# Weight buffers 32 bytes longer: the distance between the two operands of a matmul, modulo 256

## The chip, the cores and the metric

The kernel runs on one core of a Trainium2 chip. The metric is the device time of one execution in microseconds (us). Lower is better.

## The reference

Two layers of a decoder trunk on 256 positions of width 2048, in float32. What matters here is how much of it is matrix product with large weights:

```
for l in range(DEPTH):                       # 2 layers
    h = rmsnorm(x, norm_mix[l])
    z = h @ w_in[l]                          # 2048 x 2816
    q, k, v, u_ssm, z_u, z_v = split(z)
    y = concat(rmsnorm(window attention of q, k, v), rmsnorm(S5 scan of u_ssm, with ssm_w_glu),
               rmsnorm(gmlp of z_u, z_v))
    x = x + y @ w_out[l]                     # 2048 x 2048
    h = rmsnorm(x, norm_ffn[l])
    x = x + (silu(h @ w_gate[l]) * (h @ w_up[l])) @ w_down[l]   # 2048 x 5632 twice, 5632 x 2048
return rmsnorm(x, norm_final)
```

## The kernel before

**The dense products.** All large weights come as one stream of halves of 128 x 1024 float32 (512 KB). SyncE's queue brings a half into a `raw` buffer (`pump`, L172, five buffers). ScalarE copies it, rounded to TensorE's short float32 format (fp32r), into a `whi` buffer (`split_hi`, L182). VectorE subtracts: what the rounding left goes into a `wlo` buffer (`split_lo`, L191). There are four `whi` and four `wlo` buffers (`NH`), used in turn, so half number j lies in buffer j modulo 4 of each kind. The activations, transposed, are split in the same way into `xh` and `xl`, or, for the outputs of the three branches and of the FFN, into the two halves of `ya` and `yb`.

`dense` (L283) walks over the halves. A half holds two tiles of 128 x 512 (or four of 128 x 256 for the keys and values), and for each tile `unit` (L273) issues six matmuls: for each of the two blocks of 128 positions, activation-high times `whi` (L279), activation-high times `wlo` (L280), activation-low times `whi` (L281). The activation block of 128 x 128 is the stationary operand (loaded by an LDWEIGHTS of its own before each matmul), the weight tile of 128 x 512 is the moving one. After each tile `tick` lets the side work take a step: transposes (L343), attention (L817, L842, L853), the scan (L585 to L663), so that bursts of small matmuls stand between the dense ones. A half is split two to three halves ahead of its use.

**Where the buffers lie.** Tiles come from pools that lie one behind the other in a partition's memory; each tile takes a multiple of 32 bytes of each partition. First comes `const` (among its tiles, in this order: `x`, `ident`, `identr`, `consts`, `gains`, `sinks`, `nsinks`, `bs`, `dskip`, `prm` and small ones). Then the four pools of `Homes` (L135): everything that has no home of its own (`raw`, `t4`, `qT`, `kT`, `brep`, `pT` and others), then `whi` and `wlo`, then `xh`, `xl`, `ya`, `yb`, then the operands of the scan. Before the change a `whi` or `wlo` buffer has 4096 bytes, `xh` and `xl` 16384 each, and a stationary block starts a multiple of 512 bytes into its tile, a moving one a multiple of 1024. So the first `whi` lies at byte 98048, which is 383 times 256, `xh` lies 8 x 4096 bytes behind it, and the distance from any dense moving operand to any dense stationary operand is a multiple of 256. Of the other operands, `brep` starts on a multiple of 256 as well, as 11008 bytes (43 x 256) lie between its second buffer and the first `whi`; `pT`, `qT` and `kT` start 128 bytes past a multiple (4480 bytes, 17.5 x 256, lie between the first `pT` and the first `whi`).

Of the kernel before, what the change touches and what calls it, by code (L numbers as in the profile page):

```python
# [10 lines left out]
F32 = mybir.dt.float32  # L11
F32R = mybir.dt.float32r
# [3 lines left out]
L = 2  # L16
# [136 lines left out]
class Builder:  # L153
# [27 lines left out]

    def split_hi(self):  # L182
        j = self.n_hi
        h = self.work.tile([128, 1024], F32R, tag="whi", name="whi", bufs=self.NH)
        w = 512 if j < self.FINE else 1024
        for o in range(0, 1024, w):
            self.nc.scalar.activation(out=h[:, o:o + w], in_=self.raw[j][:, o:o + w], func=AF.Copy)  # L187
        self.hi[j] = h
        self.n_hi += 1

    def split_lo(self):  # L191
        j = self.n_lo
        o = self.work.tile([128, 1024], F32R, tag="wlo", name="wlo", bufs=self.NH)
        r = self.raw.pop(j)
        w = 512 if j < self.FINE else 1024
        for i in range(0, 1024, w):
            self.nc.vector.tensor_tensor(out=o[:, i:i + w], in0=r[:, i:i + w], in1=self.hi[j][:, i:i + w], op=ALU.subtract)  # L197
        self.lo[j] = o
        self.n_lo += 1
        self.pump()  # L200
# [764 lines left out]
    def build(self):  # L965
        nc = self.nc
        dr = self.dr
        cst = self.const
# [11 lines left out]
        self.gains = cst.tile([128, L, 48], F32, name="gains")  # L980
        self.sinks = cst.tile([128, L, 16], F32, name="sinks")
        self.nsinks = cst.tile([128, L, 16], F32, name="nsinks")
        self.bs = cst.tile([128, 16], F32, name="bs")[:, 0:4 * L].rearrange("p (a b) -> p a b", b=4)
        self.dskip = cst.tile([128, L, 16], F32, name="dskip")
        self.prm = cst.tile([128, 3, 32], F32, name="prm")
        self.nh = cst.tile([128, 2], F32, name="nh")
# [40 lines left out]
        for l in range(L):  # L1027
# [30 lines left out]
            a = self.acc()  # L1058
            self.dense(a, self.X, D16, ready=ready)
            self.spawn(self.attn(l, 0, a, rs))  # L1060
            a = self.acc()
            self.dense(a, self.X, D16, n=256)
            self.spawn(self.kv(a, rs))
            a = self.acc()
            self.dense(a, self.X, D16)
            self.spawn(self.attn(l, 1, a, rs))
            a = self.acc()
# [3 lines left out]
            a = self.acc()  # L1071
            self.dense(a, self.X, D16)
            self.spawn(self.gmlp_v(l, a, rs))
            a = self.acc()
# [6 lines left out]
            for t in out_tiles():  # L1081
                if t is None:
                    self.need(tssm)
                    a = []
# [24 lines left out]
            for si, s in enumerate(FF_SETS):  # L1109
                self.hev = self.events()  # L1110
                for i, c in enumerate(s):
                    a = self.acc()
                    self.dense(a, self.X, D16, ready=ready)
                    tgte = self.spawn(self.ffn_h(c, i, a, None, rs))
                    a = self.acc()
# [9 lines left out]
                for n in range(4):  # L1125
                    a = self.acc()
# [91 lines left out]
```

## Time and profile before

| what | value |
|---|---|
| runs shown | 2070.57 and 2072.56 us, median 2071.57 |
| the profiled execution: time of the run | 2073.87 us |
| its span, first to last instruction | 2072.0 us |
| granted TensorE clock, mean | 0.993 |
| busy share of the span: TensorE, its weight loads | 99%, 82% |
| VectorE, ScalarE, GpSimd | 58%, 47%, 10% |
| DMA, mean | 187 GB/s |

A row of the timeline gives the start in us from the start of the span, the duration, the engine, the line, the operation, and the tiles (output<-moving,stationary). Matmuls are pipelined: one's recorded duration is longer than the distance to the next one's start, so the pace is read from starts, and durations tell only how one compares with its like. "PEld" is a weight load, which runs beside a matmul.

### The profile page before, as it was taken

To read this page: it belongs to the slowest core of one execution; us is meant where nothing else is said; L and a number is where in the kernel's file an instruction comes from. 1 tells how busy PE (TensorE), PEld (TensorE's weight loads), DVE (VectorE), ACT (ScalarE), POOL (GpSimd) and SP (SyncE) were. 2 spreads that over 40 slices of the span, in tenths; PEclk is the share of its full clock that TensorE was granted. 3 is DMA by queue.
4 is the path that set the end of the run, shared out by engine and by line. 5 is a ranking of instruction groups with operands and counts; after the bars stand their busy time and mean duration, and the time that the engine had idled before them with its cause. 6 is when DMAs were issued, how large, how long until landed. Compare 5 with 4: busy or idle time off the path is not lost.

```text
span 2072.0 us, 25614 instructions
## 1 busy us (share of the span) xinstructions
PE 2041.6 (99%) x9728; PEld 1708.3 (82%) x9728; DVE 1210.9 (58%) x1625; ACT 969.9 (47%) x1289; POOL 206.1 (10%) x196
## 2 busy tenths in 40 slices
PE   8998999999999999999999999999999999999998
PEld 7878888888888888888888888888888888888886
DVE  6898755646555545444556796554455444554445
ACT  6555555444444443344455445544443444434444
POOL 0455004021312100000000010000000000000000
PEclk9998999999999999999999999999999999999999
DMA  7443455566656566665565455555566555555664
GB/s 247 154 142 137 131 185 187 185 217 198 219 197 218 184 219 191 193 192 188 184 218 185 148 186 182 184 189 187 191 192 193 186 192 192 189 194 186 193 194 142
DMA packets 105595, 387.98 MB, mean 187 GB/s; under 512 B 12288, under 2 KB 13056, under 8 KB 104192
## 3 DMA queue, kind: packets, MB, share of 16 engines
q1 hardware_dynamic: 105472, 386.35, 56.8%
q8 instruction: 76, 1.25, 0.2%
q14 instruction: 47, 0.39, 0.1%
HBM read 375.03 MB, written 11.27 MB: 186 GB/s over the span
## 4 chain that ended last, share of the span: by engine, by line
PE 94%; DVE 4%; issue 1%; ACT 0%; DMA 0%; SPq 0%; POOLq 0%; POOL 0%; ACTq 0%; DVEq 0%
PE acc L279 29%; PE acc L281 29%; PE acc L280 29%; PE side L343 2%; DVE wlo L197 1%; PE side L853 1%; PE side L625 1%; PE side L817 1%; DVE st L633 0%; PE side L585 0%; PE side L842 0%; PE side L663 0%; PE side L661 0%; DMA raw<-wts 0%; PE side L658 0%
## 5 line engine op out<-in xcount | busy, mean ns | idle before, releaser
L197 DVE TENSOR_TENSOR wlo<-raw,whi 128x1024 fp32r<-128x1024 f32 (+1 forms) x687 | 855.6, 1250 | 658.9 <-ACT whi L187 657.9
L187 ACT ACTIVATE whi<-raw 128x1024 fp32r<-128x1024 f32 (+1 forms) x687 | 725.8, 1058 | 971.1 <-PE acc L281 919.2
L279 PE MATMUL acc<-whi,xh 128*128 128x512 f32 (+1 forms) x1792 | 704.2, 393 | 1.9 <-ACT whi L187 1.9
L281 PE MATMUL acc<-whi,xl 128*128 128x512 f32 (+1 forms) x1792 | 693.1, 387 | 0.0
L280 PE MATMUL acc<-wlo,xh 128*128 128x512 f32 (+1 forms) x1792 | 692.6, 387 | 0.0
L281 PEld LDWEIGHTS acc<-whi,xl 128*128 128x128 f32 x1792 | 337.6, 188 | 69.4
L279 PEld LDWEIGHTS acc<-whi,xh 128*128 128x128 f32 x1792 | 337.9, 189 | 65.4 <-ACT whi L187 2.3
L280 PEld LDWEIGHTS acc<-wlo,xh 128*128 128x128 f32 x1792 | 338.1, 189 | 63.6 <-DVE wlo L197 0.4
L279 PE MATMUL acc<-whi,ya 128*128 128x512 f32 x512 | 202.0, 394 | 0.0
L280 PE MATMUL acc<-wlo,ya 128*128 128x512 f32 x512 | 199.4, 390 | 0.8 <-DVE wlo L197 0.8
L281 PE MATMUL acc<-whi,ya 128*128 128x512 f32 x512 | 199.5, 390 | 0.0
L279 PE MATMUL acc<-whi,yb 128*128 128x512 f32 x448 | 176.4, 394 | 0.0
L281 PE MATMUL acc<-whi,yb 128*128 128x512 f32 x448 | 174.6, 390 | 0.0
L280 PE MATMUL acc<-wlo,yb 128*128 128x512 f32 x448 | 174.4, 389 | 0.0
L317 POOL TENSOR_TENSOR rs<-ms,nh 128x2 f32<-128x2 f32 (+1 forms) x12 | 12.2, 1013 | 1505.9 <-DVE ms L316 1388.0
L280 PEld LDWEIGHTS acc<-wlo,ya 128*128 128x128 f32 x512 | 96.3, 188 | 20.3 <-DVE wlo L197 1.2
L281 PEld LDWEIGHTS acc<-whi,ya 128*128 128x128 f32 x512 | 96.1, 188 | 20.3
L279 PEld LDWEIGHTS acc<-whi,ya 128*128 128x128 f32 x512 | 96.2, 188 | 19.0
L281 PEld LDWEIGHTS acc<-whi,yb 128*128 128x128 f32 x448 | 84.1, 188 | 17.7
L280 PEld LDWEIGHTS acc<-wlo,yb 128*128 128x128 f32 x448 | 84.2, 188 | 16.8
L279 PEld LDWEIGHTS acc<-whi,yb 128*128 128x128 f32 x448 | 84.1, 188 | 16.8
L379 DVE SCALAR_TENSOR_TENSOR xl<-side,gains,xh 128x256 fp32r<-128x256 f32 x64 | 27.9, 480 | 44.1 <-ACT xh L377 44.1
(223 smaller groups left out, 1280.7 us busy)
## 6 DMA issues: line engine op xcount, KB each, us to landing
raw<-wts SPq DMA_DIRECT2D x684, 512.0 KB, 4.2
saved<-stash SPq DMA_DIRECT2D x4, 1792.0 KB, 6.3
stash<-saved SPq DMA_DIRECT2D x3, 1792.0 KB, 7.6
stashb<-saved SPq DMA_DIRECT2D x2, 1792.0 KB, 8.9
bc<-bc SPq DMA_DIRECT2D x8, 256.0 KB, 4.5
out<-x SPq DMA_DIRECT2D x8, 256.0 KB, 3.0
saved<-stashb SPq DMA_DIRECT2D x1, 1792.0 KB, 7.3
x<-x SPq DMA_DIRECT2D x3, 512.0 KB, 8.2
```

Of the source, the lines that this page charges most:

```text
L187: self.nc.scalar.activation(out=h[:, o:o + w], in_=self.raw[j][:, o:o + w], func=AF.Copy)
L197: self.nc.vector.tensor_tensor(out=o[:, i:i + w], in0=r[:, i:i + w], in1=self.hi[j][:, i:i + w], op=ALU.subtract)
L279: nc.tensor.matmul(out=o, lhsT=a, rhs=wh, start=first, stop=False)
L280: nc.tensor.matmul(out=o, lhsT=a, rhs=wl, start=False, stop=False)
L281: nc.tensor.matmul(out=o, lhsT=b, rhs=wh, start=False, stop=last)
L317: nc.gpsimd.tensor_tensor(out=out, in0=t, in1=self.nh[:, 0:w], op=ALU.pow)
L343: nc.tensor.transpose(ps[:, 256 * kk + 128 * m:256 * kk + 128 * m + 128], parts(2 * b + kk, m), self.ident)
L379: nc.vector.scalar_tensor_tensor(out=o, in0=src, scalar=gain[:, k:k + 1], in1=h.bitcast(F32), op0=ALU.mult, op1=ALU.subtract)
L625: nc.tensor.matmul(out=ps[:, 256 * o + 64 * g:256 * o + 64 * g + 64], lhsT=st[nm][:, 128 * g:128 * g + 128], rhs=U4[:, 4 * ct + g, :])
L817: nc.tensor.matmul(out=ps[:, nk * i:nk * i + nk], lhsT=qT[:, h0 + i], rhs=self.kT[:, j, cq, 0:nk], start=(j == 0), stop=(j == 1))
L853: nc.tensor.matmul(out=ps[:, 64 * i:64 * i + 64], lhsT=pT[:, 128 * (nb * i + b):128 * (nb * i + b) + 128], rhs=self.v[:, b, 64 * cq:64 * c ...
```

## The change

Each `whi` and `wlo` buffer is allocated with 1032 columns, of which the first 1024 are used: it takes 4128 bytes instead of 4096, so successive buffers step by 32 modulo 256. With eight of them `xh` lies 8 x 4128 = 33024 bytes (129 x 256) behind the first `whi`. Counted to any dense stationary operand, the distance modulo 256 of `whi` buffers 0 to 3 becomes 0, 32, 64, 96, and that of `wlo` buffers 0 to 3 becomes 128, 160, 192, 224 (up to the sign). The tile `bs` gets its plain shape of 128 x 2 x 4, 32 bytes where it had 64, so all that lies behind it moves down by 32 bytes; `raw`, `t4` and the rest of the first `Homes` pool then start 32 bytes lower modulo 256. No instruction is added, removed or moved.

```
@@ split_hi
-        h = self.work.tile([128, 1024], F32R, tag="whi", name="whi", bufs=self.NH)
+        h = self.work.tile([128, 1032], F32R, tag="whi", name="whi", bufs=self.NH)[:, 0:1024]
@@ split_lo
-        o = self.work.tile([128, 1024], F32R, tag="wlo", name="wlo", bufs=self.NH)
+        o = self.work.tile([128, 1032], F32R, tag="wlo", name="wlo", bufs=self.NH)[:, 0:1024]
@@ build
-        self.bs = cst.tile([128, 16], F32, name="bs")[:, 0:4 * L].rearrange("p (a b) -> p a b", b=4)
+        self.bs = cst.tile([128, L, 4], F32, name="bs")
```

## Rows read from the trace of the kernel before

**Rows 1.** The page, part 4: shares of the chain that ended last.
```profile
PE 94%; DVE 4%; issue 1%; ACT 0%; DMA 0%; SPq 0%; POOLq 0%; POOL 0%; ACTq 0%; DVEq 0%
```
**Rows 2.** Groups by shape, TensorE: line, operation, tiles, shapes, count | busy us, mean ns.
```profile
L281 PE MATMUL acc<-whi,xl 128*128 128x512 f32 x1728 | 675.0, 391 | 0.0
L280 PE MATMUL acc<-wlo,xh 128*128 128x512 f32 x1728 | 674.5, 390 | 0.0
...
L281 PE MATMUL acc<-whi,ya 128*128 128x512 f32 x512 | 199.5, 390 | 0.0
...
L281 PE MATMUL acc<-whi,yb 128*128 128x512 f32 x448 | 174.6, 390 | 0.0
...
L281 PE MATMUL acc<-whi,xl 128*128 128x256 f32 x64 | 18.1, 283 | 0.0
...
L281 PE MATMUL side<-whi,yb 128*128 128x512 f32 x16 | 6.3, 391 | 0.0
```
**Rows 3.** Timeline of TensorE, first row of an undisturbed dense stretch.
```profile
782.27 0.39 PE L279 MATMUL acc<-whi,ya 128*128 128x512 f32 x1
```
**Rows 4.** Timeline of TensorE, the row 562 matmuls later.
```profile
909.66 0.39 PE L280 MATMUL acc<-wlo,xh 128*128 128x512 f32 x1
```
**Rows 5.** Tile acc, 783 to 909 us: count, duration ns min/median/max.
```profile
L280 PE MATMUL acc<-wlo,xh x71: 389/389/389, 861.4 to 909.0; 128*128 128x512 f32 x71
L281 PE MATMUL acc<-whi,xl x70: 389/389/389, 861.6 to 908.5; 128*128 128x512 f32 x70
```
**Rows 6.** Timeline of TensorE after a burst of transposes.
```profile
289.08 0.60 PE L343 MATMUL side<-ident,x 128*128 128x128 f32 x4
289.44 0.48 PE L279 MATMUL acc<-whi,yb 128*128 128x512 f32 x1
289.75 0.40 PE L280 MATMUL acc<-wlo,yb 128*128 128x512 f32 x1
...
291.84 0.39 PE L280 MATMUL acc<-wlo,yb 128*128 128x512 f32 x1
```
**Rows 7.** Tile acc, 289.8 to 291.7 us: count, duration ns min/median/max.
```profile
L280 PE MATMUL acc<-wlo,yb x3: 387/389/396, 289.8 to 291.1; 128*128 128x512 f32 x3
L281 PE MATMUL acc<-whi,yb x3: 393/395/397, 290.0 to 291.4; 128*128 128x512 f32 x3
```
**Rows 8.** Groups at 1139.72 us: the dense matmul beside which `pT` is loaded.
```profile
L281 PE MATMUL acc<-whi,xl 128*128 128x512 f32 x1 | 0.4, 396 | 0.0
L853 PE MATMUL side<-v,pT 128*128 128x64 f32 x1 | 0.2, 221 | 0.0
```
**Rows 9.** Groups at 542.2 us: the dense matmul beside which `brep` is loaded.
```profile
L281 PE MATMUL acc<-whi,yb 128*128 128x512 f32 x1 | 0.4, 389 | 0.0
L585 PE MATMUL side<-stash,brep 128*128 128x128 f32 x1 | 0.3, 270 | 0.0
```
**Rows 10.** Groups at 144.65 us: a product of `kT` beside which `xh` is loaded.
```profile
L817 PE MATMUL side<-kT,qT 128*128 128x256 f32 x1 | 0.3, 283 | 0.0
```
**Rows 11.** Windows, 782 to 910 us: busy us (count) by engine, clock, DMA share, GB/s.
```profile
782.00:910.00 128.00, 128.00 (x566) 106.00 (x566) 65.24 (x59) 51.09 (x49) 0.00 (x0) 1.00 0.61 193
```
**Rows 12.** The page, part 5: the two splits, busy us, mean ns | idle before, releaser.
```profile
L197 DVE TENSOR_TENSOR wlo<-raw,whi 128x1024 fp32r<-128x1024 f32 (+1 forms) x687 | 855.6, 1250 | 658.9 <-ACT whi L187 657.9
L187 ACT ACTIVATE whi<-raw 128x1024 fp32r<-128x1024 f32 (+1 forms) x687 | 725.8, 1058 | 971.1 <-PE acc L281 919.2
```
**Rows 13.** The page, part 6: DMA issue of the weights, KB each, us to landing.
```profile
raw<-wts SPq DMA_DIRECT2D x684, 512.0 KB, 4.2
```

## The prediction

> **What bounds the kernel now.** I read the chain that ended last first: 94% of the span is TensorE, and no other engine has more than 4% [rows 1]. The groups by shape then say which matmuls: L279, L280 and L281 each issue 1728 + 512 + 448 + 16 matmuls of 512 columns and 64 of 256 [rows 2], where L281 stands for the three lines, that is 3 x 2704 = 8112 wide ones and 192 narrow ones, 8304 in all. So one nanosecond on each dense matmul is 8.3 us, 0.4% of the time.
>
> The pace of these matmuls is the third thing to read, and it is read from starts. In an undisturbed stretch 562 of them take 909.66 - 782.27 = 127.39 us, 226.7 ns each [rows 3, 4], and every one of them has the same duration, 389 ns [rows 5]. In that stretch TensorE is busy without a gap at a granted clock of 1.00, the 2.4 GHz level, VectorE has 65 of 128 us to do and ScalarE 51 [rows 11]. So nothing outside TensorE sets the 226.7 ns. Part of it is streaming: a matmul of 512 columns lasts 389 ns and one of 256 lasts 283 [rows 2, 5], so 256 columns cost 106 ns and 512 cost 212. The other 14.7 ns are the price of going from one matmul to the next, and that is the only thing on the bounding engine that an address can touch.
>
> The fourth thing is that this price is not fixed. After a burst of transposes the dense matmuls do not fall into the 226.7 ns at once: nine starts take 291.84 - 289.75 = 2.09 us, 232.2 ns each, 5.5 ns more [rows 6]. Their durations wander between 387 and 397 ns [rows 7] before they come to rest at 389. What these matmuls compute, and the distance of their operands, is the same as in the steady stretch; only the moment at which the stream began differs. I read this as follows: the two reads of TensorE, the moving one and the weight load that runs beside it, fall on some repeating pattern of the memory, and with all addresses equal modulo 256 the stream settles, within about ten matmuls, at a spot of the pattern that is better than the average.
>
> **What the change does, part by part.**
>
> *The distance.* No instruction changes, so the sum has one large term: 8304 matmuls times the change of the step price. Within a half, the six matmuls of a tile take `whi`, `wlo`, `whi`, `whi`, `wlo`, `whi`; after the change `wlo` lies 128 bytes (modulo 256) from its `whi`, and every half moves both on by 32. The moving address therefore changes its residue at two of three steps, and the stream never has ten equal ones in which to settle. Only matmuls with `whi` buffer 0 keep distance 0: two of three matmuls use `whi`, one buffer of four, 1/6 of all. 5/6 of 8304 is 6920.
>
> For the price the trace has two rows. First, the distance by itself: `pT`, which lies at an odd multiple of 128, is loaded beside a dense matmul of `whi`, and this one lasts 396 ns [rows 8]; `brep`, at a multiple of 256, is loaded beside one of the same kind, and this lasts 389 [rows 9]. Both loads are of 128 x 128 float32. Distance 128 costs 7 ns there. If the price grows with the distance around the ring of 256, 0 at 0 and 7 at 128, the four `whi` distances cost 0, 1.75, 3.5 and 5.25, mean 2.6, and the four `wlo` distances 7, 5.25, 3.5 and 1.75, mean 4.4. Two `whi` and one `wlo` in three give (2 x 2.6 + 4.4) / 3 = 3.2 ns, times 8304: +27 us. Second, the loss of the settled spot: 5.5 ns [rows 3, 4, 6] on 6920 matmuls: +38 us. I take the middle, +32 us.
>
> What bounds it: below, nothing forbids a gain, since 14.7 ns of each step are overhead, and if every distance but 0 removed all of it the change would be worth 6920 x 14.7 = 102 us. Above, the dearest duration seen is 397, 8 ns over 389 [rows 5, 7], which on all 8304 is +66 us.
>
> *The splits.* ScalarE writes `whi` and VectorE reads it and writes `wlo`, now at starts that are multiples of 32 instead of 256. They take 1058 and 1250 ns for a half [rows 12], and TensorE takes 12 x 226.7 = 2720 ns for it. Even at half as slow again VectorE would need 1875 ns, which with the rest of its work in the steady stretch (65 of 128 us for 47 halves, 1388 ns a half [rows 11]) comes to 2013. I cost it at nothing; TensorE's own time hides it, and without that cover a half as slow again would cost 0.6 us for each half that VectorE splits.
>
> *`raw` and the rest, 32 bytes lower.* The transfer of a half lands 4.2 us after its issue [rows 13], and five buffers at 2.72 us each are 13.6 us of room. The DMA engines are busy for 0.61 of the stretch [rows 11]. I cost this at nothing as well. If landings grew past the room, ScalarE's copy would be late next, and then L279.
>
> The sum: the profiled execution took 2073.87 us with a span of 2072.0, 2.3 above the median of the runs shown, 2071.57. 2073.9 + 32 is 2106 for it, and by the median 2071.6 + 32 = **2103 us**, +1.5%.
>
> **Rivals.**
>
> *Nothing happens* (2072 us). A product of `kT`, which lies at an odd multiple of 128, streams while `xh`, at a multiple of 256, is loaded, and it lasts 283 ns [rows 10], as do the narrow dense ones at distance 0 [rows 2]. So distance 128 costs nothing in this place, and rows 8 could owe its 7 ns to the change of operand that follows, not to the distance. Against it: the wandering of rows 6 and 7 shows that the step price depends on how the streams lie in time, and it would be odd if addresses did not enter. The Trainium skill ("SBUF — State Buffer", section "Who interferes with whom") gives TensorE two independent read ports and says that "PE and ACT never wait on anyone". By that rule distance has no price and the time stays at 2072; the trace speaks against the rule in its full width, with 387 to 397 ns for the same matmul [rows 7]. This rival also covers the case that the allocation does not give the distances that the diff asks for.
>
> *The full price everywhere* (2120 to 2140 us). If each change of residue throws the stream to a bad spot and not to an average one, every matmul pays the 7 to 8 ns of rows 7 and 8: 8304 x 7 = 58 us, 2130. It decides against my forecast where the mean step passes 231.6 ns, which is 2113 us. For it: nearly all durations of L281 in rows 7 are 393 to 397. Against it: the same stretch has a 387 too.
>
> *Faster* (about 1970 to 2030 us). Distance 0 could be the worst case, in which the two reads meet in the same place all the time; a spread would then cut into the 14.7 ns. At full effect that is 2072 - 102 = 1970, at half effect 2021; it decides from a mean step below 221.6 ns, 2030 us. For it: the overhead is there, and it is the same 14.7 ns in each of 562 steps, as a collision at a fixed distance would be. Against it: the steady 389 is near the least duration in the trace's irregular stretches (387), and the one pair at another distance in rows 8 is longer, not shorter. The Trainium skill ("TensorE: Matmul & The Clock Gate", section "Step-by-step: what each phase is for") gives 215.7 ns from start to start for 512 columns. By that figure 11 ns of each step could go, an estimate of 91 us on all 8304, 1981; no row here shows so short a step.
>
> **How the numbers follow.** Loss of the settled spot, +20 to +41 us: 0.40. Nothing: 0.20. Full price: 0.30. Faster: 0.10, of which 0.01 for less than 2%. About 2% is what a measurement of this kernel can tell from no change, 2030 to 2113 us. Slower is 0.30, within 2% is 0.40 + 0.20 + 0.01 = 0.61, faster 0.09. The likeliest case gives 2103; its own range is 2092 to 2113. The range for 8 in 10 reaches down past "nothing" to 2055, where a settling at the 387 ns of rows 7 on all matmuls would lie (8304 x 2 = 17 us less), and up to 2140, which is the 8 ns of rows 7 on all (2138); it leaves out the faster rival and the tail of the full price.
>
> **What would show it.** If I am right, the long dense stretches have a mean step of 229 to 231.6 ns where they had 226.7, and the durations of L280 and L281 there are no longer one value but several, repeating with the four buffers. The bursts of side work, the splits, and the landing of `raw` keep their durations, and TensorE stays busy without a gap between 782 and 910 us or its like. A steady 389 there would show the first rival; steps above 231.6 the second; below 221.6 the third. I am wrong in kind if the time goes anywhere else: into waits of L279 for `whi`, or of `whi` for `raw`.

## The result: 2099 us, 1.3% slower, all of it in the step between dense matmuls

The changed kernel takes 2099.38 us (median; 2099.08 to 2099.68), the kernel before 2071.57. The ratio is 1.0135, with a 95% interval from 1.0119 to 1.0152. The profiled execution has a span of 2097.2 us against 2072.0, at a mean granted clock of 0.994 against 0.993.

I read the views in the same order as before. First the shares of the chain that ended last, on the page of the changed kernel (part 4); they answer to [rows 1]:

```profile
PE 94%; DVE 4%; issue 1%; ACT 0%; DMA 0%; SPq 0%; POOLq 0%; POOL 0%; ACTq 0%; DVEq 0%
```

The row is the same, word for word: no wait has taken the place of anything, and TensorE still sets the time. Next, the two splits on the page (part 5: busy us, mean ns, idle before, releaser), which answer to [rows 12]:

```profile
L197 DVE TENSOR_TENSOR wlo<-raw,whi 128x1024 fp32r<-128x1024 f32 (+1 forms) x687 | 856.7, 1252 | 684.3 <-ACT whi L187 683.1
...
L187 ACT ACTIVATE whi<-raw 128x1024 fp32r<-128x1024 f32 (+1 forms) x687 | 724.6, 1056 | 1001.6 <-PE acc L281 945.4
```

They take 1252 and 1056 ns where they took 1250 and 1058. Both merely wait longer for the engine behind which they queue. The landing of `raw` (page, part 6: KB each, us from issue to landing) answers to [rows 13], 4.0 us where it was 4.2:

```profile
raw<-wts SPq DMA_DIRECT2D x684, 512.0 KB, 4.0
```

The window from 782 to 910 us (busy us and count for TensorE, its weight loads, VectorE, ScalarE, GpSimd; clock, DMA share, GB/s) answers to [rows 11]:

```profile
782.00:910.00 128.00, 128.00 (x560) 104.15 (x559) 62.39 (x56) 50.97 (x50) 0.00 (x0) 1.00 0.57 189
```

TensorE is busy for all 128 us at a granted clock of 1.00, as before, but gets 560 matmuls into them and not 566. So each takes longer, and the groups by shape (count, busy us, mean ns), which answer to [rows 2], say which:

```profile
L281 PE MATMUL acc<-whi,xl 128*128 128x512 f32 x1728 | 680.9, 394 | 0.0
L280 PE MATMUL acc<-wlo,xh 128*128 128x512 f32 x1728 | 680.6, 394 | 0.4 <-DVE wlo L197 0.4
...
L281 PE MATMUL acc<-whi,ya 128*128 128x512 f32 x512 | 201.4, 393 | 0.0
...
L281 PE MATMUL acc<-whi,yb 128*128 128x512 f32 x448 | 176.3, 393 | 0.0
...
L281 PE MATMUL acc<-whi,xl 128*128 128x256 f32 x64 | 18.0, 281 | 0.0
```

All wide ones are 3 to 4 ns longer, whatever their stationary operand; the narrow ones are 2 ns shorter. The pace itself is read from starts, in the timeline. Its first and last row below are the two matmuls of [rows 3] and [rows 4], again 562 steps apart; between them stands every twelfth matmul of a stretch, the first of each half:

```profile
788.33 0.40 PE L279 MATMUL acc<-whi,ya 128*128 128x512 f32 x1
...
799.42 0.40 PE L279 MATMUL acc<-whi,yb 128*128 128x512 f32 x1
...
802.22 0.39 PE L279 MATMUL acc<-whi,ya 128*128 128x512 f32 x1
...
804.97 0.39 PE L279 MATMUL acc<-whi,ya 128*128 128x512 f32 x1
...
807.74 0.39 PE L279 MATMUL acc<-whi,ya 128*128 128x512 f32 x1
...
810.51 0.40 PE L279 MATMUL acc<-whi,ya 128*128 128x512 f32 x1
...
813.30 0.39 PE L279 MATMUL acc<-whi,yb 128*128 128x512 f32 x1
...
816.06 0.39 PE L279 MATMUL acc<-whi,yb 128*128 128x512 f32 x1
...
818.83 0.39 PE L279 MATMUL acc<-whi,yb 128*128 128x512 f32 x1
...
821.60 0.40 PE L279 MATMUL acc<-whi,yb 128*128 128x512 f32 x1
...
918.15 0.39 PE L280 MATMUL acc<-wlo,xh 128*128 128x512 f32 x1
```

The 562 steps take 918.15 - 788.33 = 129.82 us, 231.0 ns each, where they took 226.7. And they repeat: four halves, one for each buffer, take 2.80, 2.75, 2.77 and 2.77 us, the next four 2.79, 2.76, 2.77 and 2.77, and 48 steps take 11.09 us each time (810.51 - 799.42 and 821.60 - 810.51). In the trace's own nanoseconds 99% of the steps of this stretch equal the step 48 places earlier within 1 ns. The durations there (tile `acc`, 800 to 905 us: count, ns min/median/max) answer to [rows 5], which had the single value 389:

```profile
L280 PE MATMUL acc<-wlo,yb x52: 388/393/398, 799.7 to 868.3; 128*128 128x512 f32 x52
...
L281 PE MATMUL acc<-whi,yb x52: 390/393/397, 799.9 to 868.5; 128*128 128x512 f32 x52
...
L279 PE MATMUL acc<-whi,yb x51: 387/394/398, 800.1 to 868.0; 128*128 128x512 f32 x51
```

Over the whole trace, the 7923 distances from the start of one wide dense matmul to the start of the next add up to 1849.6 us, and to 1820.8 before: +28.8. The rest of the span went from 251.2 to 247.6. So the whole of the 25.2 us between the two spans, and 3.6 us that came back elsewhere, is in the dense steps. Most of the 3.6 us lie between two executions and not in the change: bs_only (below), whose dense steps add up to the same 1820.8 us as before, has a rest of 248.7.

### The profile page after: what moved, and what is told of

It reads as the page before. It is cut to its first block, busy times and chain, and to the rows that moved or that the text cites. A ratio compares the mean times of both kernels' runs of the same rounds, so it can differ in the third digit from the quotient of the medians.

```text
span 2097.2 us, 25614 instructions
## 1 busy us (share of the span) xinstructions
PE 2069.7 (99%) x9728; PEld 1706.9 (81%) x9728; DVE 1211.5 (58%) x1625; ACT 968.6 (46%) x1289; POOL 204.8 (10%) x196
## 4 chain that ended last, share of the span: by engine, by line
PE 94%; DVE 4%; issue 1%; ACT 0%; DMA 0%; SPq 0%; POOLq 0%; POOL 0%; ACTq 0%; DVEq 0%
PE acc L279 29%; PE acc L280 29%; PE acc L281 29%; PE side L343 2%; DVE wlo L197 1%; PE side L853 1%; PE side L625 1%; PE side L817 1%; DVE st L633 0%; PE side L585 0%; PE side L842 0%; PE side L663 0%; PE side L661 0%; PE side L658 0%; DVE t L399 0%
## 5 line engine op out<-in xcount | busy, mean ns | idle before, releaser
L197 DVE TENSOR_TENSOR wlo<-raw,whi 128x1024 fp32r<-128x1024 f32 (+1 forms) x687 | 856.7, 1252 | 684.3 <-ACT whi L187 683.1
L187 ACT ACTIVATE whi<-raw 128x1024 fp32r<-128x1024 f32 (+1 forms) x687 | 724.6, 1056 | 1001.6 <-PE acc L281 945.4
L279 PE MATMUL acc<-whi,xh 128*128 128x512 f32 (+1 forms) x1792 | 709.9, 396 | 1.4 <-ACT whi L187 1.4
L280 PE MATMUL acc<-wlo,xh 128*128 128x512 f32 (+1 forms) x1792 | 698.6, 390 | 0.4 <-DVE wlo L197 0.4
L281 PE MATMUL acc<-whi,xl 128*128 128x512 f32 (+1 forms) x1792 | 698.9, 390 | 0.0
L281 PEld LDWEIGHTS acc<-whi,xl 128*128 128x128 f32 x1792 | 337.0, 188 | 75.9
L279 PEld LDWEIGHTS acc<-whi,xh 128*128 128x128 f32 x1792 | 337.8, 188 | 70.6 <-ACT whi L187 1.8
L280 PEld LDWEIGHTS acc<-wlo,xh 128*128 128x128 f32 x1792 | 337.5, 188 | 70.3 <-DVE wlo L197 1.2
L279 PE MATMUL acc<-whi,ya 128*128 128x512 f32 x512 | 204.0, 398 | 0.0
L281 PE MATMUL acc<-whi,ya 128*128 128x512 f32 x512 | 201.4, 393 | 0.0
L280 PE MATMUL acc<-wlo,ya 128*128 128x512 f32 x512 | 201.2, 393 | 0.0
L279 PE MATMUL acc<-whi,yb 128*128 128x512 f32 x448 | 178.3, 398 | 0.0
L281 PE MATMUL acc<-whi,yb 128*128 128x512 f32 x448 | 176.3, 393 | 0.0
L280 PE MATMUL acc<-wlo,yb 128*128 128x512 f32 x448 | 176.1, 393 | 0.0
L281 PEld LDWEIGHTS acc<-whi,ya 128*128 128x128 f32 x512 | 96.1, 188 | 22.4
L280 PEld LDWEIGHTS acc<-wlo,ya 128*128 128x128 f32 x512 | 96.2, 188 | 20.9
L279 PEld LDWEIGHTS acc<-whi,ya 128*128 128x128 f32 x512 | 96.3, 188 | 20.8
L281 PEld LDWEIGHTS acc<-whi,yb 128*128 128x128 f32 x448 | 84.1, 188 | 19.6
L279 PEld LDWEIGHTS acc<-whi,yb 128*128 128x128 f32 x448 | 84.2, 188 | 18.4
L280 PEld LDWEIGHTS acc<-wlo,yb 128*128 128x128 f32 x448 | 84.2, 188 | 18.4
```

The source lines that it names most:

```text
L279: nc.tensor.matmul(out=o, lhsT=a, rhs=wh, start=first, stop=False)
L280: nc.tensor.matmul(out=o, lhsT=a, rhs=wl, start=False, stop=False)
L281: nc.tensor.matmul(out=o, lhsT=b, rhs=wh, start=False, stop=last)
```

## The experiments

Each kernel ran beside the kernel before on the same chip; times are medians. In the diffs "before" is the base unless they say otherwise: the weight buffers have 1024 columns again. In the tables, "past" says by how many bytes modulo 256 the stationary operands lie behind the moving ones.

The expectations name theories by letters. A is the second price of the prediction: equal distances settle, changing ones lose the settled spot. B is its first price: the ring of distances, 0 at 0 and 7 ns at 128. C is that not the distance matters but the absolute place. After the first four runs they gave way to D (any distance but 0 costs the same) and E (each distance has a price of its own, and some may be as good as 0 or better), and then to F (a step costs in a mixture what its distance costs alone) and G (what counts is that the distance changes from matmul to matmul; the stream then never settles, and its step is an average whatever the distances are).

**bs_only: the absolute place alone.** The buffers as before, `bs` as in the change, so that everything behind it lies 32 bytes lower and no distance between dense operands changes.

```
+        self.bs = cst.tile([128, L, 4], F32, name="bs")
```

> Only the tile bs gets its plain shape: all that lies behind it moves down by 32 bytes, all distances between dense operands stay multiples of 256. Theory A (settling: the pace is lost when the residue of the moving operand changes from matmul to matmul) and theory B (each matmul pays for its own distance, 0 at 0 and 7 ns at 128) both expect no change, 2072 us, and a mean step of 226.7 ns in the long dense stretches. Theory C (the place of the buffers modulo 64 or 256 counts by itself, for the weight transfers or for TensorE's reads) expects the time of the changed kernel, 2099 us.

Measured: 2071.78 us, ratio 1.000 (0.999 to 1.0009). The timeline of bs_only, the same two matmuls 562 steps apart:

```profile
780.96 0.39 PE L279 MATMUL acc<-whi,ya 128*128 128x512 f32 x1
...
908.36 0.39 PE L280 MATMUL acc<-wlo,xh 128*128 128x512 f32 x1
```

127.40 us, 226.7 ns a step, as in [rows 3, 4]. C falls for the shift that the change makes, and `raw`, the splits' start addresses and the operands of the side work can be left out from here on.

**const128 and const32: one distance for all.** An unused tile ahead of `xh` moves all dense stationary operands, 128 bytes here; with 8 columns it is 32 bytes (const32).

```
-        ('xh', 'xl', 'ya', 'yb'),
+        ('padx', 'xh', 'xl', 'ya', 'yb'),
...
+        W.tile([128, 32], F32, tag="padx", name="padx")
         xh = W.tile([128, 16, 256], F32R, tag="xh", name="xh")
```

> An unused tile of 128 bytes lies ahead of xh, so that every dense moving operand is at the same distance of 128 modulo 256 from every dense stationary one. Theory A expects that the stream settles as before, since no residue changes from one matmul to the next: 2072 us, steps of about 226.7 ns. Theory B expects 7 ns on each of 8304 matmuls, +58 us, 2130 us.

> As the kernel with 128 bytes ahead of xh, but with 32: one distance of 32 for all dense matmuls. Theory A: 2072 us. Theory B: 1.75 ns on each of 8304 matmuls, +15 us, 2086 us. If the stationary operand's start at an odd multiple of 32 costs by itself (theory C), the time is above 2072 here and not with 128 bytes.

Measured: const128 2114.92 us, ratio 1.0207 (1.0192 to 1.0222); const32 2116.19 us, 1.0216 (1.0199 to 1.0233). The timeline of const128, the two matmuls 562 steps apart:

```profile
795.14 0.40 PE L279 MATMUL acc<-whi,ya 128*128 128x512 f32 x1
...
926.27 0.40 PE L280 MATMUL acc<-wlo,xh 128*128 128x512 f32 x1
```

The same two in the timeline of const32:

```profile
793.52 0.40 PE L279 MATMUL acc<-whi,ya 128*128 128x512 f32 x1
...
924.65 0.40 PE L280 MATMUL acc<-wlo,xh 128*128 128x512 f32 x1
```

Both take 131.13 us, 233.3 ns a step: 32 bytes cost as much as 128. Tile `acc` of const128, 800 to 905 us (count, duration ns min/median/max):

```profile
L280 PE MATMUL acc<-wlo,yb x61: 392/398/398, 800.3 to 875.9; 128*128 128x512 f32 x61
...
L281 PE MATMUL acc<-whi,yb x62: 392/395/398, 799.8 to 876.1; 128*128 128x512 f32 x62
```

Here the stream has settled too, onto two steps that take turns (229 and 237 ns; in const32 232 and 235). So A is wrong that equal distances settle at the old pace, and B is wrong in its shape: a quarter of the distance costs the whole price. What stands is that an address alone, with no instruction changed, moves this kernel by 43 us.

**wlo128: only the low weights at a distance.** `whi` at 0 to every stationary operand, `wlo` at 128: an unused tile of 128 bytes stands between the two kinds of buffer, another ahead of `xh`. `bs` is as in the change. (The lines of `unit` stand two further down in this kernel.)

```
-        ('whi', 'wlo'),
-        ('xh', 'xl', 'ya', 'yb'),
+        ('whi', 'pada', 'wlo'),
+        ('padx', 'xh', 'xl', 'ya', 'yb'),
...
+        if j == 0:
+            self.work.tile([128, 32], F32, tag="pada", name="pada")
...
+        W.tile([128, 32], F32, tag="padx", name="padx")
```

> bs in its plain shape, whi at distance 0 and all wlo buffers at distance 128; buffers of one kind keep one residue. The moving operand's residue changes at two of three steps, as in the changed kernel. Theory A expects about the changed kernel's time, 2090 to 2105 us, with a mean step of 230 to 231.5 ns. Theory B expects 7 ns on the third of the matmuls that use wlo, +19 us, 2091 us, with the cost on L280 alone.

Measured: 2115.22 us, ratio 1.0208 (1.0193 to 1.0223). The timeline of wlo128, the two matmuls 562 steps apart (L281, L282, L283 are the L279, L280, L281 of before):

```profile
796.61 0.40 PE L281 MATMUL acc<-whi,ya 128*128 128x512 f32 x1
...
927.74 0.40 PE L282 MATMUL acc<-wlo,xh 128*128 128x512 f32 x1
```

131.13 us, 233.3 ns a step: as slow as const128, though two of three matmuls keep distance 0. Tile `acc` of wlo128, 800 to 905 us:

```profile
L281 PE MATMUL acc<-whi,yb x63: 397/397/398, 800.1 to 877.1; 128*128 128x512 f32 x63
...
L282 PE MATMUL acc<-wlo,yb x64: 395/395/395, 799.6 to 877.3; 128*128 128x512 f32 x64
...
L283 PE MATMUL acc<-whi,yb x64: 392/392/393, 799.9 to 877.6; 128*128 128x512 f32 x64
```

A moving residue that changes at two of three steps settles all the same, on three fixed steps (236, 234, 230 ns). And the slowness isn't put down to the one that lies apart: all three lines are over 389.

**const64, const96, const160, const192, const224: the other distances.** The same edit as const128 with 16, 24, 40, 48 and 56 columns.

> One distance of 64 modulo 256 for all dense matmuls. After the kernels with 128 and with 32, theory D: the stream settles at any constant distance, on a mean step that is a whole number of 6.667 ns, 34 of them (226.7 ns) at distance 0 and 35 (233.3 ns) at any other; it expects 2115 us. Theory E: the step depends on the distance, and some distances other than 0 are as good as 0 or better; for 64 it names no number, but the time differs from 2115 us by over 10 us for one of the four distances tried here.

> One distance of 96 for all dense matmuls. Theory D expects a mean step of 233.3 ns and 2115 us. Theory E expects that one of the four distances tried here is off this by over 10 us.

> One distance with xh 192 bytes past a multiple of 256 from whi and wlo (the moving operand 64 ahead of it). Theory D expects a mean step of 233.3 ns and 2115 us. Theory E expects that one of the four distances tried here is off this by over 10 us.

> One distance with xh 224 bytes past a multiple of 256 from whi and wlo (the moving operand 32 ahead of it). Theory D expects a mean step of 233.3 ns and 2115 us. Theory E expects that one of the four distances tried here is off this by over 10 us; if the sign of the distance matters, it differs from the kernel with 32.

> The distance that is still missing: xh 160 bytes past a multiple of 256 from whi and wlo. Theory D, as the seven other distances left it: the steps settle on a sequence that repeats, and its total is a whole number of 6.667 ns; the mean lies within what the others gave, 226.7 to 234.3 ns, so 2072 to 2122 us. Theory E has no number for it. It is run to complete the table that theory F needs.

| past by | 562 steps, us | a step, ns | settles on a sequence of | time, us | ratio (95%) |
|---|---|---|---|---|---|
| 0 (before) | 127.39 | 226.7 | one step | 2071.57 | 1 |
| 32 | 131.13 | 233.3 | two | 2116.19 | 1.0216 (1.0199 to 1.0233) |
| 64 | 131.13 | 233.3 | two | 2116.47 | 1.0217 (1.0202 to 1.0232) |
| 96 | 131.67 | 234.3 | seven | 2122.1 | 1.0244 (1.0227 to 1.0261) |
| 128 | 131.13 | 233.3 | two | 2114.92 | 1.0207 (1.0192 to 1.0222) |
| 160 | 131.13 | 233.3 | three | 2117.54 | 1.0218 (1.0203 to 1.0233) |
| 192 | 128.64 | 228.9 | three | 2085.53 | 1.0067 (1.0052 to 1.0082) |
| 224 | 131.13 | 233.3 | four | 2115.26 | 1.0210 (1.0195 to 1.0225) |

The two that differ, from the timeline of const96:

```profile
795.23 0.40 PE L279 MATMUL acc<-whi,ya 128*128 128x512 f32 x1
...
926.90 0.40 PE L280 MATMUL acc<-wlo,xh 128*128 128x512 f32 x1
```

and from that of const192:

```profile
786.73 0.39 PE L279 MATMUL acc<-whi,ya 128*128 128x512 f32 x1
...
915.37 0.39 PE L280 MATMUL acc<-wlo,xh 128*128 128x512 f32 x1
```

Tile `acc` of const192, 800 to 905 us (count, duration ns min/median/max), shows what a short sequence looks like; each line has one duration of its own:

```profile
L279 PE MATMUL acc<-whi,yb x49: 394/394/394, 799.8 to 865.7; 128*128 128x512 f32 x49
...
L280 PE MATMUL acc<-wlo,yb x49: 388/388/388, 800.0 to 865.9; 128*128 128x512 f32 x49
...
L281 PE MATMUL acc<-whi,yb x49: 392/392/392, 800.2 to 866.2; 128*128 128x512 f32 x49
```

D falls on 192 and 96. E holds in that a distance has a price of its own (192 is 30 us off D's 2115); that another distance is as good as 0 none of the seven shows. Distance 0 is the best of the eight, 192 is next, and the ring is not symmetric: 64 and 192 lie equally far from 0 and differ by 31 us.

const224 beside bs_only settles theory C as well. In both, the stationary operands start 224 bytes past a multiple of 256. In bs_only the moving ones start there too, in const224 on a multiple of 256, and const224 takes 43 us more. So the distance counts, and not the place of the stationary operands.

The column of steps is also a column of whole numbers. The difference of 233.33 and 226.67 is 6.67 ns; in that unit they are 35 and 34, 228.9 is 34 1/3 (103 units for its three steps), and 234.3 is 35 1/7 (246 for its seven).

**swap: the change with the two kinds of buffer exchanged.** `wlo` at 0, 32, 64, 96 and `whi` at 128 to 224, counted as in the change (0, 224, 192, 160 and 128, 96, 64, 32 past), on the changed kernel. The use of the `wlo` buffers also moves one place round, so `whi` and `wlo` of a half are paired in another way than in the change.

```
     def split_hi(self):
         j = self.n_hi
+        if j == 0:
+            self.work.tile([128, 1032], F32R, tag="wlo", name="wlo", bufs=self.NH)
```

> The changed kernel with the two kinds of weight buffers in the other order in memory: wlo first, then whi, each 32 bytes longer, and the use of the wlo buffers one place further round. Now whi, which two of three matmuls stream, has xh 128, 96, 64 and 32 past it, and wlo 0, 224, 192, 160. Theory F (a table: each matmul pays the mean step that its distance has when it is the only one) expects (2 x 233.5 + 230.5) / 3 = 232.5 ns, 5.8 over the kernel before, +48 us, 2120 us. Theory G (what counts is that the residue changes from matmul to matmul; the stream never settles, and the step is an average over bad and good spots whatever distances there are) expects the changed kernel's 231.0 ns, 2099 us.

Measured: 2103.56 us, ratio 1.0151 (1.0136 to 1.0166). The timeline of swap, the two matmuls 562 steps apart (L281 and L282 are L279 and L280 of before):

```profile
792.66 0.40 PE L281 MATMUL acc<-whi,ya 128*128 128x512 f32 x1
...
922.74 0.39 PE L282 MATMUL acc<-wlo,xh 128*128 128x512 f32 x1
```

130.08 us, 231.5 ns. By F, with `whi` twice and `wlo` once in three, the table gives (2 x 233.55 + 230.55) / 3 = 232.55, where 233.55 is the mean of the table for 32 to 128 and 230.55 that for 0, 160, 192 and 224. The measured step is 1 ns under it, and only 0.5 ns above that of the changed kernel, which G named. But the stream does settle, on 48 steps that repeat, and the time is 4 us above G's 2099.

**halfstep: a whole half at one distance.** `whi` and `wlo` of a half lie behind one another in one tile of 2056 columns, so the twelve matmuls of a half keep one distance, which is 0, 224, 192 and 160 past for the four buffers; they are used in the order 0, 160, 192, 224. An unused tile of 128 bytes behind them (not shown) keeps `xh` at 0. `bs` is as in the change.

```
+        pair = self.work.tile([128, 2056], F32R, tag="wpair", name="wpair", bufs=self.NH)
...
+        h = pair[:, 0:1024]
...
+        o = self.pair.pop(j)[:, 1024:2048]
```

> The two kinds of weight buffers as halves of four common tiles, each 32 bytes longer: whi and wlo of a half of the stream have the same residue, so all twelve matmuls of a half have one distance, and the distance moves on by 32 with each half: xh 0, 224, 192, 160 past them. Theory F expects the mean of these four, (226.7 + 233.3 + 228.9 + x) / 4 with x from the kernel with 160 of the same job; with x between 226.7 and 234.3 that is 228.9 to 230.8 ns, 2090 to 2106 us. Theory G, if each change of residue throws the stream off for about ten matmuls, expects 231 to 232 ns, 2108 to 2116 us.

Measured: 2104.06 us, ratio 1.0154 (1.0137 to 1.0171). The timeline of halfstep, the two matmuls 562 steps apart (L283 and L284 are L279 and L280 of before):

```profile
790.89 0.39 PE L283 MATMUL acc<-wpair,ya 128*128 128x512 f32 x1
...
921.04 0.39 PE L284 MATMUL acc<-wpair,xh 128*128 128x512 f32 x1
```

130.15 us, 231.6 ns. F's mean over the four distances is 230.55, 1 ns less; G said 231 to 232, but its 2108 to 2116 us are too much. Where the 1 ns lies, the steps within a half show. The timeline of halfstep, a half at distance 0: its first matmul, its seventh, and the first of the next half:

```profile
821.49 0.39 PE L283 MATMUL acc<-wpair,yb 128*128 128x512 f32 x1
...
822.87 0.39 PE L283 MATMUL acc<-wpair,yb 128*128 128x512 f32 x1
...
824.23 0.40 PE L283 MATMUL acc<-wpair,yb 128*128 128x512 f32 x1
```

The first six steps take 1.38 us, 230 ns each, the other six 1.36 us, 226.7 each, which is the pace of the kernel before. The half at 192 that starts at 815.93 us comes to the three durations of const192, 388, 392 and 394 (tile `acc` of halfstep, 817.1 to 818.6 us):

```profile
L284 PE MATMUL acc<-wpair,yb x3: 392/392/392, 816.9 to 818.2; 128*128 128x512 f32 x3
L285 PE MATMUL acc<-wpair,yb x3: 394/394/394, 817.1 to 818.5; 128*128 128x512 f32 x3
...
L283 PE MATMUL acc<-wpair,yb x2: 388/388/388, 817.3 to 818.0; 128*128 128x512 f32 x2
```

In the trace's own nanoseconds, averaged over the halves of the long stretch, each half runs on the steps that its distance has alone: from its seventh step at 0, its eighth at 160, its fourth at 192 and 224. So twelve equal distances are long enough. What F lacks is the change of distance, which puts the stream off for three to seven steps. Over a half this costs 25 ns at 0, 15 at 160, 13 at 192 and -5 at 224, on average 12 ns, 1 ns a step.

**xl128: two stationary operands at two distances.** `xl` alone lies 128 bytes further; `xh`, `ya` and `yb` stay at 0, and so does every moving operand. `bs` is as in the change.

```
-        ('xh', 'xl', 'ya', 'yb'),
+        ('xh', 'padx', 'xl', 'pady', 'ya', 'yb'),
...
+        W.tile([128, 32], F32, tag="padx", name="padx")
         xl = W.tile([128, 16, 256], F32R, tag="xl", name="xl")
+        W.tile([128, 32], F32, tag="pady", name="pady")
```

> bs in its plain shape, xl alone 128 bytes off: the moving operand keeps one residue, the stationary one of every third matmul of the products with xh and xl (5376 of 8304) lies at distance 128; those with ya and yb stay at 0. Theory F expects (2 x 226.7 + 233.1) / 3 = 228.8 ns in these products, +2.1 ns, +11 us, 2083 us. Theory G expects about the step of the kernel with wlo alone at 128, 233.0 ns, there, +6.3 ns on 5376 matmuls, +34 us, 2106 us. Both expect 226.7 ns in the products with ya and yb. If L280 is the longer one, the weight load that runs beside the matmul counts; if L281, its own.

Measured: 2089.81 us, ratio 1.0084 (1.0069 to 1.0099), which neither F's 2083 nor G's 2106 foresaw. The timeline of xl128, a stretch of products of `xh` and `xl`, two matmuls 162 steps apart:

```profile
871.98 0.39 PE L279 MATMUL acc<-whi,xh 128*128 128x512 f32 x1
...
909.42 0.39 PE L279 MATMUL acc<-whi,xh 128*128 128x512 f32 x1
```

37.44 us, 231.1 ns a step. Tile `acc` of xl128, first L280 of the products of `ya` (800 to 858 us), then the three lines of the products of `xh` and `xl` (872 to 910 us):

```profile
L280 PE MATMUL acc<-wlo,ya x48: 389/389/389, 800.0 to 853.7; 128*128 128x512 f32 x48
...
L279 PE MATMUL acc<-whi,xh x55: 389/389/389, 872.0 to 909.4; 128*128 128x512 f32 x55
...
L280 PE MATMUL acc<-wlo,xh x55: 396/396/396, 872.2 to 909.6; 128*128 128x512 f32 x55
...
L281 PE MATMUL acc<-whi,xl x56: 397/397/397, 871.7 to 909.9; 128*128 128x512 f32 x56
```

In one and the same execution the products of `ya` keep 389 ns and those of `xh` and `xl` don't. It is L280, beside which `xl` is loaded, and L281, which uses it, that grow, by 7 and 8 ns; the matmul between two `xh` stays at 389. F's table gives (2 x 226.7 + 233.3) / 3 = 228.9 for these products, 2.2 ns too little: one operand of three at a distance costs here two thirds of what all at this distance cost (4.4 of 6.7 ns), and in wlo128 all of it. G's 233.0 is 1.9 ns too much. So neither F nor G stands.

## Why the prediction was right, and where its reasons were not

**What bounds the kernel: right.** TensorE's dense step, and nothing else. The chain, the splits, the landing and the gapless window are as forecast, and the mean step of 231.0 ns lies in the forecast 229 to 231.6. The edits costed at nothing cost nothing: bs_only, which has the second of them alone, differs by 0.0% (-0.1 to +0.1), and the splits kept their durations within 2 ns.

**The distance has a price: right, and the rival "nothing" falls.** const128 has all residues equal and one distance other than before, and takes 43 us more. The rule of the Trainium skill that spoke for this rival ("SBUF — State Buffer", section "Who interferes with whom": TensorE and ScalarE never wait on anyone) differs from the measurement here, if it is read as saying that the place of TensorE's operands is free: 226.7 ns a step become 233.3 by an unused tile of 32 or 128 bytes. Whether one of its two reads waits for the other or something else lies behind it, no run tells.

**The size of the step: right within its bounds.** Forecast were 32 us on 8304 matmuls, 3.9 ns each, between 3.2 (the ring) and 4.6 (5.5 ns on 5 of 6). Measured in the undisturbed stretch are 231.0 - 226.7 = 4.3 ns. The time did not grow by 8304 x 4.3 = 36 us, but by 27.8, and the steps show most of the reason. Counted from the last break (a burst or a step of over 300 ns) in the two traces, the first five average 231.6 ns before and 232.7 after, the sixth to twelfth 228.0 and 231.9, and the 6300 later ones 226.7 and 231.0. Near a burst the matmuls had been slow before as well [rows 6]: this takes about 3 us from the 36. The 381 dense matmuls that are not followed by another wide one, the narrow ones among them, take another 1.6 us from it, and the steps of over 300 ns account for about 2 more. The constant distances have the same proportion: const128 has 6.7 ns more in its settled step, 55 us on 8304, and took 43; const192 has 2.2, 18.5 us, and took 13.8. About three quarters of what the settled step says arrives in the time. The prediction overlooked this, and its price was a little low, so the two errors partly cancelled: 2103 forecast, 2099 measured. That the step came out so near is in part luck: of the two prices whose middle was taken, one rests on a ring that is wrong, the other on a settling that was thought lost.

**"The stream never has ten equal ones in which to settle": wrong in what was drawn from it.** Equal distances do not bring the old pace back: const128 has them and stays at 233.3 ns. And the changed stream settles too, onto 48 steps that repeat with the four buffers; wlo128 settles on three, const128 on two. Every arrangement tried comes to rest in a sequence that repeats, of one to seven steps where the distances repeat with each tile, of 48 where they repeat with the four buffers. Its sum is a whole number of 6.67 ns: 1663 units for the 48 steps of the change, 1666 for swap, 1667 for halfstep, 104 for the three steps of xl128. So the loss isn't that settling stops. It settles at a worse sum: 34 units a step, which is what before has, is the least of any sequence tried. One part of the idea holds: in halfstep each change of distance puts the stream off for three to seven steps. How much of the change's 4.3 ns is such changing, and how much the distances themselves, no run separates. The prediction had read the settled spot of before as better than the average; that holds, for another reason.

**"`wlo` lies 128 bytes (modulo 256) from its `whi`, and every half moves both on by 32": wrong, without an effect on the sums.** In the program as built, the `whi` buffers are used in the order 0, 3, 2, 1 and the `wlo` buffers in the order 0, 3, 1, 2, not half j in buffer j modulo 4. Four halves in turn have `whi` and `wlo` 0 and 128, 160 and 32, 192 and 96, 224 and 64 bytes past. The eight distances still occur equally often, which is all that the two prices use.

**"Only matmuls with `whi` buffer 0 keep distance 0", and so pay nothing: wrong.** They keep the distance and not the step. In the trace of the changed kernel the settled steps of L279 and L281 on this buffer average 230.4 and 232.7 ns, not 226.7. wlo128 shows the same in the open: `whi` at 0, and no line left at 389.

**The price by the ring: wrong.** Linear from 0 to 128 was my choice without a row behind it. 32 bytes cost 6.7 ns and not 1.75, the mean over the seven distances other than 0 is 6.2, and 192 costs 2.2. That the sum (3.2 ns) came close to 4.3 is chance. Rows 8, though, from which the end of the ring was taken, were read aright: 7 ns more beside an operand at 128 [rows 8, 9], and const128's settled step is 6.7 ns longer. The pair was a typical one: in the whole trace of before the last wide matmul ahead of a load of `pT` lasts 396 ns in 12 of 20 cases, ahead of a load of `brep` 389 ns in 11 of 14. Rows 10, which spoke for no price, show one short matmul of 256 columns, and such do not carry this price: in the changed kernel the narrow ones became 2 ns shorter, and the mean step between two of them went from 121.3 to 119.7 ns.

**The other rivals.** The full price everywhere is what a single other distance does: six of the seven constant distances ended at 2115 to 2122 us. The change stays under it. That two thirds of its moving operands are `whi`, whose distances include the two cheap ones, 0 and 192, explains little of this: swap gives these to `wlo` and has a step only 0.5 ns longer. By the table alone its step would be 231.55, which is near the 231.0 measured; but the same sum misses wlo128 by 4.4 ns, xl128 by 2.2, swap and halfstep by 1, so the table gives the direction and isn't the mechanism. The faster rival needed a step below 221.6 and found none: no arrangement had a settled mean below 226.7. The Trainium skill's 215.7 ns ("TensorE: Matmul & The Clock Gate", section "Step-by-step: what each phase is for") is reached by no run here: the least settled step is 226.7.

**What stays open.** Why the sums are whole multiples of 6.67 ns, why 192 is nearly as good as 0 and 64 is not, which accesses meet, and by what rule distances that change combine. Distances that aren't multiples of 32 were not tried, nor other lengths of matmul or types. No arrangement tried beats the kernel before.

## What to carry to other kernels

When TensorE is the bound and its matmuls come back to back, where the operands lie can matter: here it was worth up to 2.4%. Try an unused tile of 32 to 224 bytes between the two pools, and read the step from starts hundreds of matmuls apart, in a stretch without side work. Equal distances of a multiple of 256 were the best here; spreading the addresses over all residues did not average anything out in its favour, since most distances cost by themselves, a change of distance puts the stream off for some steps, and the pace of a mixture isn't the mean of its parts. Here about three quarters of the settled difference arrived in the time, because bursts break the stream. Measure before believing a table of single distances.

## What the runs showed of the hardware that was not expected

- Back-to-back matmuls of 512 columns, each with a weight load, settle at 226.7 ns with both operands on the same residue modulo 256, and at 228.9 to 234.3 with the stationary one 32 to 224 bytes past; a shift of both by 32 bytes costs nothing (bs_only).
- A stream settles on steps whose sum over one repetition is a whole number of 6.67 ns. Single steps within them range from 224 to 241 ns (both in halfstep).
- A stationary operand at another residue lengthens two matmuls, the one beside which it is loaded and the one that uses it: 396 and 397 ns against 389, with steps of 232.3 and 234.3 against 226.7 (xl128).
- After a change of distance a stream needs three to seven steps until it has the pace of the new one (halfstep).
